# Gate tiles 2 to 7 of the linear-attention branch in three pairs of seven products

## The chip, the cores and the metric

The kernel runs on one core of a Trainium2 chip. The metric is the device time of one execution in microseconds (us); the figure given for a kernel is the median of several executions. Besides, one execution is recorded by the hardware profiler: its span runs from the first to the last instruction, and the trace lists every instruction of the five engines with start and duration: TensorE (PE, its weight loads apart as PEld), VectorE (DVE), ScalarE (ACT), GpSimd (POOL) and SyncE (SP, which issues the DMAs).

## The reference, cut to what matters

One layer of a hybrid decoder in fp32, between two half-step SwiGLU networks. The middle part, the mixer, has two branches, linear attention (a) and stick-breaking attention (b):

```
proj = u @ w_in                       # u: 560 tokens x 1024
q_a, k_a, v_a, gk_low, r_a, q_b, k_b, v_b, gate_a, gate_b = jnp.split(proj, offs, axis=-1)
...
o_a = rms_norm(o_a, gla_norm_g).reshape(B, L, V_GLA).astype(x.dtype) * jax.nn.silu(r_a)
...
o_b = sb_attend(q_b, keys, vals, sb_bias, q_off).reshape(B, L, SB_W)
m = jax.nn.sigmoid(gate_a) * (o_a @ w_o_gla) + jax.nn.sigmoid(gate_b) * (o_b @ w_o_sb)
h = h + rms_norm(m @ w_out, mix_post_g)
```

The change concerns `r_a`, 1024 columns of `u @ w_in`: the gate of the linear branch. They are computed in eight tiles of 128 columns, r0 to r7, each for all tokens (512 prompt tokens, 32 sample tokens and 16 meta tokens, 560 in all).

## The kernel before

**Products.** Activations lie transposed, 128 features on the partitions and the tokens in two halves, columns of 280 and 264. Every fp32 factor is split into a high part (hi) and the rest (lo), and a product is the sum of hi·hi, hi·lo and lo·hi. A **plain** tile (`tile_steps`, L718) takes 8 steps, one for each 128 rows of the weight, of 6 matmuls (three products, two token halves; lines 728, 729 and 731). A **pair** (`seven_steps`, L1043) computes two neighbouring tiles at once in the manner of Strassen: seven products of half depth and half width in place of eight, each with 4 x 3 matmuls, so 84 matmuls in 14 steps where two plain tiles take 96 in 16 (lines 1079, 1080 and 1081). Its four accumulators a, d, b and c are all the PSUM banks for such products. In between, intermediate sums are carried over: ACT copies a to b (L1069) before the third product, which is the first to use b, later b to c (L1069 again), and to SBUF (L1059).

**Weights.** A weight arrives by DMA as `raw`, ACT casts it to `hi` (L1006 or L706), DVE subtracts to get `lo` (L172 with `lo<-raw,hi`). A pair needs sums of weight quarters besides: `weights_at` (L1036) sets four DVE additions of 128x512 (`weight_sums`) 10, 10, 9 and 8 steps before the pair, and the parts b1, t, b2 and t4, each a cast and a subtraction, from 6 steps before to 6 steps after its beginning (b1 4 and 3 steps before when a pair stands ahead of it).

**What follows a gate tile.** `gate_r` (L2358), after a plain tile: the attention output `o` comes back from DRAM, ACT takes the sigmoid of both accumulators (L2371), DVE multiplies (`by`, three L172), then `o` is split: a cast on ACT (L2345) and a subtraction on DVE. `r_pair` (L2384) does the same for a pair at steps 13 to 16 after its beginning (`by_t`, `by_sg`; ACT lines 2399, 2414, 2403 and 2345). All split `o` are the input of the tiles o0 to o7 (`out_a`).

**Order.** Each engine executes its instructions in the order in which the program emits them. The list `MIXER` (L44) gives the order of the mixer's tiles, "R" for a plain tile, "S" for a pair. A counter of steps runs along, and other work hangs on fixed steps: `later(n, f)` emits f n steps further on, `when(n, f)` at an absolute step. The first 24 steps run inside `attention`, among the pieces for the last pair of heads: scores (L2010), scans (L2027), weighing (128x1343, L172), copies of the turned weights (L2089 on PE, L2092 on ACT) and sums (L2105). Steps after those are laced with the sample tokens' attention: keys turned (L2192 on PE, L2194 on ACT), products (L2206, L2239, L2293, L2308), and softmax pieces on DVE (L2252, L2253, L2277, L2278). All those are at fixed step numbers, whichever tile runs there. SBUF is an arena of rooms whose places are read from the table `PLACES`, one byte for each taking; an instruction that writes a room taken over waits for those that used it last.

Of the kernel before, what the change touches and what calls it, by code (L numbers as in the profile page):

```python
# [18 lines left out]
KD = D // P  # L19
# [31 lines left out]


PLACES = bytes.fromhex("""
1e1218555a06420c505e52908e8070488a7a7e667668946a3264868c4c7c6038842a883462283c742672240a544e6e000292042c4a6c78823e2c
103c383a363047412d54565a0a5808443e424660067c8c0c34882c4c26247262842a742e1e0200146e824a786c123016921a36226a664890947a
32683c8e1e1880408a5a701003254e64277e86360e1a050428761b3e8a1f3a2318535c1c64360265700019260c0d4e1b017176283b5a64180038
3924231e0270190c1a36770d4e1876535b04013822715a5d641f1e0c1a707718100219384e712176645c1e0c5a702353100077183971763b6421
1e0c4e705323105a380c1a717776183a64651e23703818534e100e0c7684946c90788e6458468274167c7a4c500a88183c123008684a8c442c48
2e9270747a242a361e2c004c5a5d4823502e2036424b222a1e214b4d222a4c202d50511e4b5150224d1f201e212400301e50181c224b38373b36
393a19181b82667468603c5c14123e160690625a42501c442e4618887a84802d1b7e76947857153f6961673d928c0a72221e08200d4a13758317  # L60
49704c484b4d5d548e865c8a6e566a0e2d6c0c2c7c401910645570801a2a18847a54585c57562d888978795494725856768c0a2c187e9220221e
0428887824269046003234304e743a6862186053146612023b364a4c3f3e0848162c8209395c1e9238787e2a5a3626765618424c3c245d685428
4a60538c48666394881a14623f3e3a72501c22291e045d926078384a30342a2c7e58680a234e905c486654823a8c08282409636294885b551674
4604480032222047535a3e601e7802382e4a50665d429236194e3a5c764c9063088c82091c625e5672943c745b182e3846025406287e78926636
262458304c4a6888901676631214343a5b4e2b193802302a4e460a08573644555854423a3430061902265b2b425534522438503b262a060a5430
1b364e3a02192450570844425b2b19364e3402525618080a4630242e26292a2c4250380654025b1942242e34572938521a1c2c36024e30502a06
0a2d5b5d083418582c2a42245b072e38245256291c1806342a503a02542608240a4e3028504345341a3628065b2b4e420a303a0656072c2a3738
241c1934265402283a0845365c305e432e1a24454e37075b30585642062a2c1843191b4536383a5434025e5c1d4f565158282e0a0618424e5b08
0230024345560642262434580a36545c5e3a381c34360a1a58062e2c3a184f515e06323058011a54004a4c5c185e5a76622a28604a44423a3856
3e4e460234081c62560a60763663064a4c32625c525036185a5e320002463a441d08364a38421c4c345c0604621c080676604c56440a185c3a5a  # L70
1c0832065e424438585c08301a360a3a4c1c4656544b1a3208344a5d5c3022061e5848204a4442385c3a340b1a460a44080642304c1c32480a1e
203a54585632481a4a2c34634476602a246150280a26020462060801004460522200762e30634c1c02184e3e5a604246621a4a4c635e004d0405
18026260364b44764a4d395a18006e64108a1612687c787e6a740c7a408e8c88707284576726941e926d3406083266800a2c4a37829150140e4c
668648206c54828356242a28903a36573c8c60623e3d662d82804a37670822762c6e8e64661e339226670635949532080b8872706655847a0774
54610c0d41403f7e68426f0a778d658f46588a0706080b16124f747c3830548a104c3a780e423648866c267a142a9084822e5a1a24804a7e7288
683462662c2001187092527658604e5450563e466e0c7a5b8e1d65641a1e1c8c320822245a4243065f7a943d0402203c46181c26648f451e0008
225c1a03441f4006233c0a8f478e2028642400422202441c433c40235a03041a64245d0b5c0a461e5f42008f8e653e5a3d20040b64400226245c
4625416544428f3c0a8e40210222645c0425652400448f3c208e47400a0241465c5d5e24648e668874606c386834842e7e8a042c901800200e76
3c827c5430620a48725c0846108636784e5e06042818261e015c245a064600035c25282700245a05290403260424030025292826274206544e04
40033e241d28041a3c002c52137a8c18261c  # L80
""")


class Arena:
# [52 lines left out]
def hybrid_step(  # L137
# [15 lines left out]
    V, S, G, T = nc.vector, nc.scalar, nc.gpsimd, nc.tensor  # L153
# [64 lines left out]
    r = 0  # L218
# [47 lines left out]
    W1 = NP + NS - HW  # L266
# [452 lines left out]
    def tile_steps(act, w1, order=range(KD)):  # L719

        wid = (HW, w1)
        hi, lo = st.parts.pop(0)
        acc = {h: ps("acc") for h in range(2)}
        for k in order:
            a = {h: act.get(k, h, wid[h]) for h in range(2)}
            for h in range(2):
                w = HW if k == order[0] else wid[h]
                T.matmul(acc[h][:, :w], hi[k], act.get(k, h, w)[0], start=(k == order[0]), stop=False, skip_group_check=True)  # L728
# [36 lines left out]
    def later(n, f):  # L765
        todo.append([n, f])
# [748 lines left out]
    with tc.manual_schedule(engines={E.PE, E.DVE, E.Activation, E.Pool}):  # L1515
# [262 lines left out]
        for e in range(2):  # L1778
            acc = {h: ps("acc") for h in range(2)}
# [14 lines left out]
        for j in range(5):  # L1794
            n = P if j < 4 else NTL
# [31 lines left out]
        for hd, head in enumerate(HEADS):  # L1827
# [10 lines left out]
            for c in range(2):  # L1838
# [495 lines left out]
    oas, oap = Parts(), []  # L2334
# [163 lines left out]
    with tc.manual_schedule(engines={E.PE, E.DVE, E.Activation, E.Pool}):  # L2498
        kps, mixer_at, at = {}, {}, {}

        def when(n, f, *args):
            mixer_at.setdefault(n, []).append((f, args))
# [54 lines left out]
        for pr in range(8):  # L2557
            now, n, after = Pair(pr), BEGIN[pr + 1], BEGIN[pr + 2] if pr < 7 else BEGIN[8] + 18
# [25 lines left out]
        n, w0 = BEGIN[8], Weights(0)  # L2584
# [16 lines left out]
        n = 0  # L2601
# [29 lines left out]
        n = 8 * len(PAGES)  # L2631
# [43 lines left out]
        n = 0  # L2675
# [18 lines left out]
        for i, (n, h) in enumerate([(n, 0) for n in range(8)] + [(n, 1) for n in range(7, -1, -1)]):  # L2694
# [12 lines left out]
            acc = product(ms, (h,), held[n])  # L2707
# [94 lines left out]
```

## Time and profile before

| | |
|---|---|
| median of 3 executions | 1482.21 us (1482.03 to 1482.53) |
| the profiled execution's own time | 1483.2 us |
| its span | 1481.5 us |
| mean granted TensorE clock | 0.999 |
| ACT busy | 818.8 us (55%) |
| POOL busy | 86.6 us (6%) |
| r0, r1, r2 and r7 begin | 777.7, 789.1, 800.6 and 811.9 us |
| pairs r3 and r5, tile o0 begin | 820.4, 835.4 and 850.3 us |

The profiled execution took 1.0 us more than the median, and its span leaves out 1.7 us of it. The gate tiles occupy 778 to 850 us; the last pieces of attention run among them up to about 812 us. In the listings a time is the start in us from the span's beginning; then follow the length, engine, line, operation, output and inputs, the tile's shape, and in brackets how long the engine had stood idle and for what. Rows of matmuls overlap each other: their pitch, not their length, is what one costs.

### The profile page before, as it was taken

How to read it: one execution, taken by the hardware profiler on the slowest of the kernel's cores; microseconds unless marked ns; L12 is line 12 of the kernel's file. 1: busy time of each engine (PE TensorE's matmuls, PEld its weight loads, DVE VectorE, ACT ScalarE, POOL GpSimd, SP SyncE). 2: the span in 40 equal slices, each digit the busy share in tenths (PEclk: the TensorE clock that was granted, in tenths of full speed). 3: DMA queues.
4: the chain of work that ended last, by engine and by line, in shares of the span. 5: the costliest groups of instructions: out<-in, count | busy, mean ns of one | idle time of the engine just before them, and what ended most of it. 6: DMA issues, size and time to landing. Idle time of an engine off the chain costs nothing.

```text
span 1481.5 us, 29805 instructions
## 1 busy us (share of the span) xinstructions
PE 1472.6 (99%) x11825; PEld 1426.8 (96%) x11825; DVE 1097.5 (74%) x1844; ACT 818.8 (55%) x1537; POOL 86.6 (6%) x175
## 2 busy tenths in 40 slices
PE   9999999999999999999999999999999999999998
PEld 8999999999999889999998999999999999999998
DVE  5888888855677866988887754776577888889544
ACT  7455545533565557777776544644564554545334
POOL 2000000000000111412211000000000000000000
PEclk9999999999999999999999999999999999999999
DMA  8133333324665787568687757335531333333243
GB/s 254 44 100 92 100 94 100 90 79 128 179 133 130 180 164 162 115 116 154 148 141 168 238 130 212 100 93 156 164 104 51 104 95 110 96 104 88 85 141 123
DMA packets 288541, 187.61 MB, mean 127 GB/s; under 512 B 10988, under 2 KB 266674, under 8 KB 288402
## 3 DMA queue, kind: packets, MB, share of 16 engines
q1 hardware_dynamic: 280706, 181.97, 46.5%
q0 software_dynamic: 7680, 3.74, 2.3%
q8 instruction: 93, 1.52, 0.4%
q14 instruction: 46, 0.38, 0.1%
q10 hardware_dynamic: 16, 0.00, 0.0%
HBM read 160.63 MB, written 25.03 MB: 125 GB/s over the span
## 4 chain that ended last, share of the span: by engine, by line
PE 95%; DVE 2%; ACT 1%; DMA 1%; issue 0%; DVEq 0%; SPq 0%; ACTq 0%
PE acc L1302 8%; PE acc L1301 8%; PE acc L1300 8%; PE acc L741 7%; PE acc L744 6%; PE acc L742 6%; PE acc L728 5%; PE acc L729 5%; PE acc L731 5%; PE acc L1079 4%; PE acc L1081 4%; PE acc L1080 4%; PE acc L1242 2%; PE acc L1239 2%; PE acc L1240 2%; PE ps L2105 1%
## 5 line engine op out<-in xcount | busy, mean ns | idle before, releaser
L172 DVE TENSOR_TENSOR room<-room,room 128x560 fp32r<-128x560 f32 (+14 forms) x464 | 300.9, 667 | 85.2 <-ACT room L1059 17.7
L172 DVE TENSOR_TENSOR lo<-raw,hi 128x1024 fp32r<-128x1024 f32 (+1 forms) x207 | 248.6, 1202 | 76.6 <-ACT hi L1006 39.3
L1302 PE MATMUL acc<-room,lo 128*128 128x280 f32 (+1 forms) x896 | 259.6, 290 | 0.0
L1300 PE MATMUL acc<-room,hi 128*128 128x280 f32 (+1 forms) x896 | 259.1, 289 | 0.0
L1301 PE MATMUL acc<-room,hi 128*128 128x280 f32 (+1 forms) x896 | 259.1, 289 | 0.0
L1006 ACT CAST hi<-raw 128x1024 fp32r<-128x1024 f32 x114 | 119.5, 1052 | 143.5 <-PE acc L1301 49.0
L728 PE MATMUL acc<-room,hi 128*128 128x280 f32 x608 | 173.1, 301 | 0.3 <-DVE room L175 0.3
L1300 PEld LDWEIGHTS acc<-room,hi 128*128 128x128 f32 x896 | 168.8, 188 | 0.0
L1302 PEld LDWEIGHTS acc<-room,lo 128*128 128x128 f32 x896 | 168.7, 188 | 0.0
L1301 PEld LDWEIGHTS acc<-room,hi 128*128 128x128 f32 x896 | 168.5, 188 | 0.0
L729 PE MATMUL acc<-room,hi 128*128 128x280 f32 x608 | 163.5, 288 | 0.0
L1079 PE MATMUL acc<-room,hi 128*128 128x280 f32 x476 | 141.7, 298 | 1.1 <-ACT acc L1069 1.0
L172 DVE TENSOR_TENSOR lo<-room,hi 128x1024 fp32r<-128x1024 f32 x106 | 101.2, 955 | 53.0 <-ACT hi L1006 52.8
L1081 PE MATMUL acc<-room,lo 128*128 128x280 f32 (+1 forms) x476 | 138.5, 291 | 0.0
L1080 PE MATMUL acc<-room,hi 128*128 128x280 f32 (+1 forms) x476 | 138.2, 290 | 0.0
L706 ACT CAST hi<-raw 128x1024 fp32r<-128x1024 f32 (+1 forms) x93 | 93.6, 1007 | 77.6 <-issue 20.4
L1006 ACT CAST hi<-room 128x1024 fp32r<-128x1024 f32 x106 | 89.1, 840 | 81.7 <-PE acc L1301 60.6
L731 PE MATMUL acc<-room,lo 128*128 128x280 f32 x608 | 125.7, 288 | 0.0
L728 PEld LDWEIGHTS acc<-room,hi 128*128 128x128 f32 x608 | 114.4, 188 | 5.3 <-issue 3.9
L729 PEld LDWEIGHTS acc<-room,hi 128*128 128x128 f32 x608 | 114.6, 188 | 0.3
L741 PE MATMUL acc<-room,hi 128*128 128x280 f32 (+2 forms) x388 | 110.7, 295 | 0.0
L742 PE MATMUL acc<-room,hi 128*128 128x280 f32 (+2 forms) x388 | 108.8, 290 | 0.0
(412 smaller groups left out, 3588.2 us busy)
## 6 DMA issues: line engine op xcount, KB each, us to landing
raw<-in_w_in_dram SPq DMA_DIRECT2D x68, 256.0 KB, 5.2
raw<-in_ffn_w_gate_dram SPq DMA_DIRECT2D x64, 256.0 KB, 3.1
raw<-in_ffn_w_up_dram SPq DMA_DIRECT2D x64, 256.0 KB, 3.3
raw<-in_ffn_w_down_dram SPq DMA_DIRECT2D x36, 448.0 KB, 3.8
raw<-in_w_in_dram SPq DMA_DIRECT2D x29, 512.0 KB, 6.9
out_dram<-room SPq DMA_DIRECT2D x36, 256.0 KB, 4.0
room<-in_cache_k_dram SPq DMA_DIRECT2D x32, 256.0 KB, 5.1
room<-in_cache_v_dram SPq DMA_DIRECT2D x32, 256.0 KB, 5.9
```

Of the source, the lines that this page charges most:

```text
L172: (eng or V).tensor_tensor(out=out, in0=a, in1=b, op=op)
L728: T.matmul(acc[h][:, :w], hi[k], act.get(k, h, w)[0], start=(k == order[0]), stop=False, skip_group_check=True)
L729: T.matmul(acc[h][:, : wid[h]], hi[k], a[h][1], start=False, stop=False, skip_group_check=True)
L731: T.matmul(acc[h][:, : wid[h]], lo[k], a[h][0], start=False, stop=(k == order[-1]), skip_group_check=True)
L741: T.matmul(acc[h][:nw, : wid[h]], wh, a[h][0], start=(k == 0), stop=False)
L742: T.matmul(acc[h][:nw, : wid[h]], wh, a[h][1], start=False, stop=False)
L1006: S.copy(hi[:, :kt], src)
L1079: T.matmul(x[:, :n], hi, act_[k][0][:, :n], start=(first and k == 0), stop=False, skip_group_check=True)
L1081: T.matmul(x[:, :w], lo, act_[k][0][:, :w], start=False, stop=(k == 3), skip_group_check=True)
L1300: T.matmul(x[:, :QW], hi, act[k][0], start=(first and k == 0), stop=False, skip_group_check=True)
L1301: T.matmul(x[:, :QW], hi, act[k][1], start=False, stop=False, skip_group_check=True)
L1302: T.matmul(x[:, :QW], lo, act[k][0], start=False, stop=(k == 3), skip_group_check=True)
```

## The change

The list `MIXER` now begins with r0 and r1 plain and three pairs, r2 with r3, r4 with r5 and r6 with r7; before it was r0, r1, r2 and r7 plain and two pairs, r3 with r4 and r5 with r6. The gate tiles take 16 + 42 = 58 steps where they took 32 + 28 = 60. Two further lines follow from that: o0 takes its eight inputs in another order, so that those of the last pair come last, and the second halves of the normed input's rooms are given back at the beginning of r2's pair. `PLACES` is replaced as a whole: from the first byte on, tiles lie in other rooms.

```
-MIXER = [("R", "r", 0), ("R", "r", 1), ("R", "r", 2), ("R", "r", 7), ("S", "r", 3), ("S", "r", 5)]
+MIXER = [("R", "r", 0), ("R", "r", 1), ("S", "r", 2), ("S", "r", 4), ("S", "r", 6)]
...
 PLACES = bytes.fromhex("""
-1e1218555a06420c505e52908e8070488a7a7e667668946a3264868c4c7c6038842a883462283c742672240a544e6e000292042c4a6c78823e2c
+2a005a300e38084434161254701a806a72784a487c18267e944c64625666884e8e527a6e608c1f281c8a680c0d3682923c403e4e6c905824204e
...
-        acc = yield from tile_steps(oas, W1, (0, 1, 2, 7, 3, 4, 6, 5) if n == 0 else range(KD))
+        acc = yield from tile_steps(oas, W1, (0, 1, 2, 3, 4, 5, 7, 6) if n == 0 else range(KD))
...
-        when(starts["r", 3], halved)
+        when(starts["r", 2], halved)
```

What moves on the engines is seen at three places. The names in the rows: `raw`, `hi` and `lo` are weights, `acc` the accumulators, `ps` other PSUM tiles, `room` a place of the arena; in brackets stands which engines or DMA queues the instruction waits for.

The first place is DVE while r1 runs, from the `lo` of r1's weight to the weighing of the last but one head. Before:

```order
L172 TENSOR_TENSOR lo_9276<-raw_8897,hi_9275 128x1024 [waits DMAHW2_49,PE_49,Activation_49]
L2027 SCALAR_TENSOR_TENSOR room_81_4592<-room_81_4592,room_103_5552 128x400
L2027 SCALAR_TENSOR_TENSOR room_81_4592<-room_81_4592,room_103_5552 128x528 [waits Activation_49]
L2027 SCALAR_TENSOR_TENSOR room_5_73<-room_5_73,room_103_5552 128x144 [waits Activation_49]
L172 TENSOR_TENSOR room_76_4272<-acc_9223,room_76_4272 128x280 [waits Activation_49]
L172 TENSOR_TENSOR room_76_4272<-acc_9224,room_76_4272 128x264 [waits Activation_49]
L172 TENSOR_TENSOR room_131_7980<-room_131_7980,room_76_4272 128x544 [waits DMAHW5_49,DVE_49]
L172 TENSOR_TENSOR room_139_9071<-room_139_9071,room_81_4592 128x1343 [waits Pool_49]
```

And now:

```order
L172 TENSOR_TENSOR lo_9275<-raw_8894,hi_9274 128x1024 [waits DMAHW2_49,PE_49,Activation_49]
L172 TENSOR_TENSOR room_131_7063<-raw_9201,raw_9040 128x512 [waits DMAHW7_49,DMAHW1_49]
L172 TENSOR_TENSOR raw_9040<-raw_9040 128x512 [waits DMAHW0_49,DVE_49]
L172 TENSOR_TENSOR room_131_7063<-raw_9201,raw_9040 128x512 [waits DMAHW3_49,DVE_49,PE_49]
L2027 SCALAR_TENSOR_TENSOR room_84_4595<-room_84_4595,room_92_5119 128x400
L2027 SCALAR_TENSOR_TENSOR room_84_4595<-room_84_4595,room_92_5119 128x528 [waits Activation_49]
L172 TENSOR_TENSOR room_9_112<-raw_9201,room_131_7063 128x512 [waits DMAHW4_49,DMAHW0_49,DMAHW6_49,DVE_49,PE_49]
L2027 SCALAR_TENSOR_TENSOR room_74_4270<-room_74_4270,room_92_5119 128x144 [waits Activation_49]
L172 TENSOR_TENSOR room_85_4596<-acc_9222,room_85_4596 128x280 [waits DMAHW6_49,DMAHW5_49,Activation_49]
L172 TENSOR_TENSOR room_85_4596<-acc_9223,room_85_4596 128x264 [waits Activation_49]
L172 TENSOR_TENSOR room_108_5557<-room_108_5557,room_85_4596 128x544 [waits DMAHW6_49,DVE_49]
L172 TENSOR_TENSOR room_105_5535<-room_105_5535,room_84_4595 128x1343 [waits Pool_49]
```

The four sums for the pair at r2 now stand between the scans and ahead of r0's three multiplications and the weighing, in a queue that held none of them there.

The second place is ACT a few steps into r2, around the copies of the last head's turned weights (L2092). Before:

```order
L2092 COPY room_133_8271<-ps_9476 128x512 [waits DMAHW4_49,PE_49]
L2092 COPY room_5_73<-ps_9482 128x384 [waits DVE_49,PE_49]
L2092 COPY room_5_73<-ps_9487 128x384 [waits PE_49]
L2371 ACTIVATE room_135_8642<-acc_9342 128x280 [waits DMAHW7_49]
L2371 ACTIVATE room_135_8642<-acc_9343 128x264
L2092 COPY room_139_9071<-ps_9532 128x512 [waits PE_49,Pool_49]
```

And now:

```order
L1006 CAST hi_9465<-room_131_7063 128x1024
L2092 COPY room_131_7063<-ps_9484 128x512 [waits DVE_49,PE_49]
L2092 COPY room_65_3345<-ps_9490 128x384 [waits DMAHW4_49,PE_49]
L2092 COPY room_99_5423<-ps_9495 128x384 [waits DMAHW3_49,PE_49]
L1006 CAST hi_9510<-raw_9201 128x1024 [waits DMAHW7_49,DMAHW0_49]
L2371 ACTIVATE room_9_112<-acc_9345 128x280 [waits DMAHW5_49]
L2371 ACTIVATE room_9_112<-acc_9346 128x264
L1069 COPY acc_9515<-acc_9513 128x280 [waits DVE_49,PE_49]
L2092 COPY room_131_7063<-ps_9549 128x512 [waits PE_49]
```

The first copy now writes the room of the pair's weight sum t, so it comes after the `lo` of t on DVE (which reads that room, and follows the last head's weighing there). A cast of 128x1024 and the pair's copy of a to b have come in ahead of the copy from ps_9549, and the copy of a to b waits for DVE, which still reads that bank for r1's gate.

The third place is ACT where one pair follows on another. Before (r3 to r5), from r3's last copy to the copy of a to b for r5:

```order
L2414 COPY room_103_5552<-acc_9809 128x264 [waits PE_49]
L1006 CAST hi_10003<-raw_9720 128x1024 [waits DMAHW5_49,DMAHW4_49]
L2403 ACTIVATE room_135_8642<-room_103_5552 128x544 [waits Activation_49]
L2345 CAST room_145_10033<-room_131_7980 128x544 [waits DVE_49,Pool_49]
L1069 COPY acc_10008<-acc_10006 128x280 [waits PE_49]
```

And now (r4 to r6; the like stands between r2 and r4):

```order
L2414 COPY room_141_9719<-acc_9802 128x264 [waits PE_49]
L1006 CAST hi_9998<-raw_9735 128x1024 [waits DMAHW7_49,DMAHW0_49]
L2403 ACTIVATE room_84_4595<-room_141_9719 128x544 [waits Activation_49]
L2194 COPY room_75_4271<-ps_10017 128x512 [waits PE_49]
L2194 COPY room_75_4271<-ps_10023 128x512 [waits PE_49]
L2345 CAST room_145_10036<-room_85_4596 128x544 [waits DVE_49]
L1069 COPY acc_10003<-acc_10001 128x280 [waits PE_49]
```

The chain ahead of the copy is the same, with two key copies more in it; it stands at two places now in place of one.

More of the change, by code (lines that the diff above doesn't have):

```diff
@@ L58 @@
[L58 to L77, printed above, removed]
@@ L78 @@
-4625416544428f3c0a8e40210222645c0425652400448f3c208e47400a0241465c5d5e24648e668874606c386834842e7e8a042c901800200e76
-3c827c5430620a48725c0846108636784e5e06042818261e015c245a064600035c25282700245a05290403260424030025292826274206544e04
-40033e241d28041a3c002c52137a8c18261c
+2a005a300e38084434161254701a806a72784a487c18267e944c64625666884e8e527a6e608c1f281c8a680c0d3682923c403e4e6c905824204e
+4213748476860c154f220a38061e100e4e0c6266208856446e8c607a30528e081c28688a2a3e3c908292246c58000204862b5c3684761a542674
@@ new lines @@
+4c187c6438427e4a794e528071785a13953c402c447215316a3a37483e5c3879734f80327850422b2a702d30154494716b145e4e3b365a795c2f
+80525d2a42787071145094364413796a3a465e5a728095782e2a14367094436a3a2c815a5e15446b782e45361372736a9442715a806b15793a5e
+783644726a73705c9536136b943a785a8180157270447305006a9436383a78688860746e4c647a80627c6c03139286548c1e0c728a2670062428
+1a3432306c4e18461c022a44278013812546425a19042444244326454702424624424444424547464244434447545a0c2c2a4353181b44464345
+4247194f51703a882282742a36343094386a24407e483c280626805262667c18924f6c8a8c0851354e202123788464861e322d2b4a713b758937
@@ new lines @@
+9513312f832a1503608e026e720b68904d7a764c801a041892131c7c3e4a1566621402080a0b4d4c8d04130a8a84146c640286784c8c5400585a
+5c5e10824e262c0c56042e240e6a2a5288347013209422322b7446423a363b7830444c371f1e545a5134404a7e88704e0882525e64268c740a50
+78028d948a203a10424684366d6c5848142a1e13343c5144023e5a2e4024545c4a8674781f7e2c8c940a8a100e203b4c26373a360c428d13566a
+8b883c0a14523e1e5a590434506c2806947e440e582010705b265e8a648c4e8233020032488316842a6a2e2c4d4c56281f12063a30867e946c08
+38364a42408c70748a786482100c4e165425485b44468413244d320e1f06222042125e4e08288430165b54371f48445d46424e08244d300e3612
@@ new lines @@
+385e5b092846061684323a4e54481f5b36424409260684324d244a3848470712164e0e305c4c1f423654485e163b26060e325b4e42460744124c
+4a092457551684305b5e361f48541228225d24060e3209161f845e07424e465b4457554d36383a1630845e281f48543712442409480630325d84
+4c5b260728164e3a423846364c202224840e26365b541f4212384a06090e304757484c84424e28163a542436565e265c44328446081f485b5424
+361206264c484a088407300e46443a4238284e1656461f4236544484325b5c21163a28380a584414122423064e27822654583a4064365a8c1614
+04345c284a084c8c8249445e0a884838162656221f6436145a4644485c5a88423a405854200a6421381f145a5e5c28084a48203638644c280838
@@ new lines @@
+0a1622565840543a082636065a1f145e4e5c58163a24120a2809264021083a223812161736243e501e5e1416525a583c08225c5d1e3a12385e20
+363e5052140a2826405c245e5a521e2208323a4a48094c82640e8c88841404653012164244083836320a843a6431654234228850081e203e5446
+64653032443f4254640a064e3e08425035512a3054101a6446704492687a9476781c6e620c006690607e248a747c72806c8648186a8b4a82164c
+4f2853403c3e048b140e8e6c8c4e53525a025e5c282724061e363884084e82168a124b534f88221a3a0a104e187c6a724a4887860c004f53908c
+80744e7e666160486362781d791c6e7a426811013b0b0d4664701b898569284e42202460924a7094265250043e6c140e662c3c025a5c5e8e1632
@@ new lines @@
+562a6a18828a7a6e727e7c12423054806474228c903886361e0646103a58484c350a633c8869001c302b6884852d44781a0c564607634a3e3469
+084b497962883c064254784a33844058082a636968562c89444c78793e420684302e3f8859620a2b544a0878896848474332422a79304c63542e
+6284853e58694488424a68782a633008624b85545643446842843e782e883062893f85544a08433e424446687884889062705c387a6c7c7e3654
+24660872428c8e300e5012046074945e86441e8a82926e3c2220542c06584872562a7442862f2e5654201e21222a1f2375745458201f75231e21
+74224254121e3c74413022873d343f063c26640832868e8c6c
```

3 lines of the change are left out of this document (removed).

## The prediction

> **What bounds the kernel now.** I read the page's list of engines first, then the waits of PE over the whole run, then stretches of 10 us around the gate tiles, and last the rows of PE, DVE and ACT there. The page:
>
> ```profile
> PE 1472.6 (99%) x11825; PEld 1426.8 (96%) x11825; DVE 1097.5 (74%) x1844; ACT 818.8 (55%) x1537; POOL 86.6 (6%) x175
> ```
>
> And the first two groups of PE's waits (in all, times, longest):
>
> ```profile
> PE acc L1533 <- DVE own L276: 1.1, 1, 1.1
> PE acc L1079 <- ACT acc L1069: 1.0, 1, 1.0
> ```
>
> PE sets the time, and in the mixer it waits only once, 1.0 us where pair r5 follows pair r3. So a matmul less is gained in full, and any new wait is paid in full. Whether new waits come depends on the engines beside PE, in the stretches where the change puts work (start:end, then the length, and busy time of PE, PEld, DVE, ACT and POOL; at the end clock, DMA share and GB/s):
>
> ```profile
> 780.00:790.00 10.00, 10.00 (x75) 8.59 (x75) 4.51 (x7) 6.95 (x13) 2.97 (x6) 1.00 0.38 84
> 790.00:800.00 10.00, 10.00 (x88) 9.60 (x90) 8.43 (x16) 6.77 (x12) 1.30 (x6) 1.00 0.83 237
> 800.00:810.00 10.00, 10.00 (x144) 7.88 (x134) 7.79 (x12) 5.89 (x15) 1.62 (x4) 1.00 0.75 184
> 810.00:820.00 10.00, 10.00 (x85) 9.97 (x84) 9.66 (x30) 6.92 (x14) 1.24 (x6) 1.00 0.79 194
> 820.00:830.00 10.00, 10.00 (x124) 9.11 (x123) 9.35 (x21) 4.26 (x9) 0.00 (x0) 1.00 0.95 261
> ```
>
> DVE has some 4 us free between 790 and 810 (20 - 8.43 - 7.79 = 3.8) and almost nothing from 810 to 830. That is where the first of the three pairs now runs, and this is the point on which the forecast turns.
>
> **What PE saves.** Starts of equal steps give the pitch:
>
> ```profile
> 810.40 0.29 PE L728 MATMUL acc<-room,hi 128*128 128x280 f32 x1
> 811.15 0.29 PE L728 MATMUL acc<-room,hi 128*128 128x280 f32 x1
> ...
> 825.35 0.29 PE L1079 MATMUL acc<-room,hi 128*128 128x280 f32 x1
> 826.12 0.29 PE L1079 MATMUL acc<-room,hi 128*128 128x280 f32 x1
> ...
> 829.58 0.28 PE L1079 MATMUL acc<-room,hi 128*128 128x264 f32 x1
> 830.29 0.28 PE L1079 MATMUL acc<-room,hi 128*128 128x264 f32 x1
> ```
>
> A plain step is 811.15 - 810.40 = 0.75, a pair's step 0.77 with 280 columns and 0.71 with 264. A pair has ten of the first and four of the second: 10 x 0.77 + 4 x 0.71 = 10.5; the two plain tiles that it replaces take 16 x 0.75 = 12.0. With the longer first matmul after each interleave I take **-1.3**, between -1.2 (all at 0.77) and -1.5.
>
> **What DVE gets.** One pair more brings four sums (128x512) and the subtractions of t and t4; b1 and b2 stand for the two plain weights' own. The rows of DVE before, around r1 and r2:
>
> ```profile
> 786.61 1.23 DVE L172 TENSOR_TENSOR lo<-raw,hi 128x1024 fp32r<-128x1024 f32 x1 [1.36 <-ACT hi L706]
> 787.76 2.58 DVE L2027 TENSOR_TENSOR_SCAN room<-room,room 128x400 f32<-128x400 f32 x3
> 790.36 0.79 DVE L172 TENSOR_TENSOR room<-acc,room 128x280 f32<-128x280 f32 x2
> 791.19 2.19 DVE L172 TENSOR_TENSOR room<-room,room 128x544 f32<-128x544 f32 x2
> 793.41 0.33 DVE L2038 COPY room<-room 128x96 f32<-128x96 f32 x2
> ...
> 794.37 0.29 DVE L172 TENSOR_TENSOR room<-ps,room 32x128 fp32r<-32x128 f32 x1
> 796.09 0.73 DVE L172 TENSOR_TENSOR room<-room,room 128x544 fp32r<-128x544 f32 x1 [1.43 <-ACT room L2345]
> 796.73 1.60 DVE L2027 TENSOR_TENSOR_SCAN room<-room,room 128x272 f32<-128x272 f32 x2
> ...
> 800.72 1.56 DVE L172 TENSOR_TENSOR room<-room,room 128x1343 f32<-128x1343 f32 x1
> ...
> 809.46 0.69 DVE L172 TENSOR_TENSOR room<-raw,raw 128x512 f32<-128x512 f32 x1 [0.56 <-PE ps L2105]
> ```
>
> A 128x1024 `lo` costs 787.76 - 786.61 = 1.15, a sum about 0.7, so the extra work is 4 x 0.7 + 1.15 + 0.6 = 4.5 us, the last term being t4 with half the columns. It must fit between 787 and 812, where the free time is a handful of short waits for ACT. I follow the queue as it stands now, from the `lo` of r1, which should begin at 786.61 as before: `lo` to 787.8, three sums and the fourth among the scans (2.6 + 2.8) to 793.2, r0's three products and the weighing (0.8 + 2.2) to 796.2, six small copies 1.2 (793.41 to 794.66) to 797.4, `lo` of b1 to 798.5, the split of r0 (0.7) to 799.2 against 796.8 before. Three scans (2.8, which is 796.73 to 800.72 less a `lo` between) to 802.0, the last weighing 1.6 and its copies 0.4 to 804.0, the `lo` of t to **805.1**.
>
> **What waits behind it.** ACT and PE rows of the same place:
>
> ```profile
> 795.92 2.08 ACT L2194 COPY room<-ps 128x512 f32<-128x512 f32 x4
> ...
> 802.37 0.86 ACT L2092 COPY room<-ps 128x384 f32<-128x384 f32 x2 [2.70 <-DVE room L172]
> 803.11 0.70 ACT L2371 ACTIVATE room<-acc 128x280 f32<-128x280 f32 x2
> ...
> 805.40 1.06 ACT L706 CAST hi<-raw 128x1024 fp32r<-128x1024 f32 x1
> ...
> 805.38 0.76 PE L2239 MATMUL ps<-room,room 128*32 128x32 f32 x64
> ```
>
> Two waits are added here. The L2194 copies now write a room that r0's split reads, so they start at 799.2 in place of 795.92, and PE's products with the sample tokens come late by about 2. Then L2092 writes the room of t and waits for its `lo`: 805.1 in place of 802.37. Behind it in ACT's queue: three L2092 (0.52 as each of the four L2194 above, and 0.75 for the two of 384) to 806.4, the cast of b2 (0.95) to 807.3, two sigmoids (0.6) to 807.9, the copy of a to b (0.4), which waits besides for DVE's product on r1's bank (after the `lo` of b2, 807.3 + 1.15 + 0.4 = 808.9) to 809.3, and the next L2092 (0.5) to 809.8. PE's L2239, which the copied weights feed a little further on in PE's queue, cannot pass its own wait for that copy: 809.8 against 805.38, **+4.4**. The bounds: 0, if DVE's short waits take up the 4.5 us, and 5.5, if every one of those hops costs 0.1 more.
>
> **Where pair follows on pair.** Before, that is r3 to r5:
>
> ```profile
> 835.41 0.29 PE L1079 MATMUL acc<-room,hi 128*128 128x280 f32 x1
> ...
> 837.13 0.38 ACT L2414 COPY room<-acc 128x264 f32<-128x264 f32 x1
> ...
> 840.76 0.64 ACT L2345 CAST room<-room 128x544 fp32r<-128x544 f32 x1 [1.75 <-DVE room L172]
> 841.31 0.39 ACT L1069 COPY acc<-acc 128x280 f32<-128x280 f32 x1
> ...
> 841.75 0.40 PE L1079 MATMUL acc<-room,hi 128*128 128x280 f32 x1 [1.00 <-ACT acc L1069]
> ```
>
> The old pair's last gate, sigmoid, product and cast, all stand in ACT's queue ahead of the copy of a to b; that chain takes 841.75 - 835.41 = 6.34 from the new pair's beginning. PE was late by only 1.0 because L2206 and L2293 (1.9 us together) ran among its first four steps. At r4 to r6 those are not there, only one L2192 (0.8): 4 x 0.77 + 0.8 = 3.9 of cover, so PE waits 6.34 - 3.9 = **+2.4**, and the old 1.0 is gone, **-1.0**. At r2 to r4 another wait comes first:
>
> ```profile
> 811.52 0.18 DVE L175 SCALAR_TENSOR_TENSOR room<-room,newm 128x32 f32<-128x32 f32 x1
> 813.21 0.68 DVE L172 TENSOR_TENSOR room<-raw,room 128x512 f32<-128x512 f32 x1
> ...
> 819.82 0.86 DVE L2277 COPY room<-ps 128x32 f32<-128x32 f32 x8
> 820.61 0.27 DVE L2278 COPY room<-ps 32x128 f32<-32x128 f32 x1
> ...
> 821.22 0.64 PE L2308 MATMUL ps<-room 64*32 64x128 f32 x16
> ...
> 823.67 0.40 PE L1079 MATMUL acc<-room,hi 128*128 128x280 f32 x1
> ```
>
> L2308 needs the copy L2278, which before was done 0.34 ahead of it. Now L2278 stands behind r3's first gate product, and that behind the cast of r2's: r2's fifth product ends six steps and some keys (6.5) before r4 begins, and from there stand in a row a copy on ACT (0.4), two subtractions on banks (0.8), two softmax groups (813.21 - 811.52 = 1.7 each), `lo` of b1 and t (2 x 1.15), three products (3 x 0.65), two sets of L2277 and L2278 (819.82 to 820.88, 1.05 each), and two instructions of ACT between (0.9): 11.8. By that count L2278 ends 5 after r4's beginning, and three steps (2.3) are all that PE has before it: **+2.6**; then the copy of a to b for r4 another **+0.4**. The nearest row gives the lower bound: a chain of 6.34 against a cover of four steps and L2308, L2206 and L2293 (2.45, 821.22 to 823.67) gives 0.8 for both.
>
> **The sum**: -1.3 + 4.4 + 2.6 + 0.4 + 2.4 - 1.0 = +7.5 on 1483.2 for the profiled execution, 1490.7; less the 1.0 by which that stood over the median, 1489.7. The hops were all taken as coming one behind the other; where one is off, it will rather be that two waits cover each other, as L2308 does with r4's copy. I forecast **1489**. After o0 nothing gives time back, since PE has no waits there to lose. The new order of o0's inputs costs nothing as long as r6's two splits come within o0's last two steps, six steps (4.5) after its beginning; else the difference. The halved rooms cost nothing, they add no instruction. The new places of the arena add waits anywhere; outside the gate tiles I cost them at nothing, bounded by -0.5 (a wait such as L744's or L872's goes) and +2 (two waits such as r5's come).
>
> **Rivals.**
>
> 1. *DVE takes the sums in its short waits* (the other side: not slower). The place is the `lo` of t; if it ends by 802.4, where L2092 went before, ACT's queue is as early as it was, r4's chain is shorter by as much, and what remains is -1.3 with the wait between pairs twice at 1.0 in place of once: 1483.2 - 1.3 + 1.0 - 1.0 = 1481.9 on the median's scale, down to 1480.9 with both covered. For it: 3.8 us free from 790 to 810, and 5.5 from 780 to 790 if the sums could go there. Against it: they stand behind r1's `lo` at 786.61, which waits for its cast.
> 2. *Only the waits of the pairs come.* The backlog at r2 is eaten by the waits of DVE, but pair on pair is as counted: -1.3 + 0.8 to 3.0 + 2.4 - 1.0 gives +0.9 to +3.1 on the median, 1483.1 to 1485.3.
> 3. *Worse than counted.* From 820 to 830 the DMA queues are at 0.95; the first raw quarters are now fetched earlier and r2's outputs come back in that stretch. A load that lands 2 us late behind r4 gives about 1491.5.
> 4. *The clock.* In every stretch above PE's granted clock is 1.00, and no wait was over 1.1 us. If a wait of 2.6 halved it for as long again, four steps would take 0.77 more each: +2.6, so 1491.6. The Trainium skill (TensorE: Matmul & The Clock Gate, "Why this matters for your kernels") warns of PE idle for more than about 3 us, after which the clock is halved; no run here shows so long a pause yet, and by that rule the waits counted above stay just short of it.
> 5. *The change does not save what it says*: were a pair's steps slower beside the attention pieces (0.80 in place of 0.77), -1.3 would be -0.9; this moves the sum by 0.4.
>
> **Chances.** The forecast (waits of both kinds, 1486 to 1491) 0.53; rival 2 0.2; rival 1 0.13; rivals 3 and 4 together 0.14; rival 5 lies in the range of each. The range must reach into rival 1 and a little beyond the forecast: 1481.3 to 1491.7. About 0.2%, or 3 us, is what a measurement of this kernel can tell from no change: faster is below 1479.2, slower above 1485.2. Faster has 0.03, from rival 1 with a wait lost elsewhere; the rest of rival 1 and most of rival 2 are the same, 0.27; slower 0.7.
>
> **What would show it.** In the trace after: PE's waits should list L2239 or its neighbours behind ACT L2092 at about 806 to 810, L2308 behind DVE L2278, and L1079 behind ACT L1069 two times rather than once; DVE between 790 and 810 near 9.5 of 10; o0 beginning near 857 in place of 850.34. If PE shows no wait between 795 and 810, rival 1 or 2 holds, and my count of DVE's queue is wrong. If waits stand there but the total is 1482, something later gave time back. A granted clock under 1.00 after a wait speaks for rival 4.

## The result, and the profile after

The changed kernel takes 1493.54 us (median of 6 executions, 1491.82 to 1494.75) where the kernel before took 1482.12 beside it: the ratio is 1.0076, with a 95% interval of 1.0063 to 1.0089. It is slower by 11.4 us; the forecast was 1489, and the range ended at 1491.7. The profiled execution took 1491.82, with a span of 1490.1 and a mean granted clock of 0.998. The page's list of engines:

```profile
PE 1474.0 (99%) x11813; PEld 1426.2 (96%) x11813; DVE 1102.1 (74%) x1850; ACT 821.7 (55%) x1544; POOL 87.7 (6%) x175
```

PE has 12 matmuls less and yet is busy for 1.4 us longer than before (1472.6). The span grew by 8.6, so that the other 7.2 are new idle time. The waits of PE say where (in all, times, longest):

```profile
PE acc L1079 <- ACT acc L1069: 2.5, 1, 2.5
PE ps L2308 <- DVE room L2278: 2.1, 1, 2.1
PE ps L2239 <- ACT room L2092: 1.8, 1, 1.8
...
PE ps L2192 <- DVE room L172: 0.8, 1, 0.8
...
PE ps L2089 <- ACT room L2092: 0.7, 1, 0.7
PE ps L2089 <- ACT room L2194: 0.5, 1, 0.5
```

These six are 8.4 us, all in the gate tiles, where there was one of 1.0. The stretches of 10 us (PE, PEld, DVE, ACT and POOL; at the end clock, DMA share and GB/s) show the rest:

```profile
790.00:800.00 10.00, 8.73 (x70) 8.17 (x68) 9.83 (x18) 4.94 (x9) 0.91 (x3) 1.00 0.52 137
800.00:810.00 10.00, 7.49 (x64) 6.04 (x64) 8.10 (x11) 6.05 (x13) 0.11 (x1) 1.00 0.80 228
...
820.00:830.00 10.00, 7.90 (x94) 6.94 (x96) 8.97 (x29) 5.90 (x11) 0.11 (x1) 1.00 0.72 210
830.00:840.00 10.00, 9.98 (x103) 9.56 (x93) 8.06 (x14) 5.69 (x12) 0.00 (x0) 1.00 0.67 215
840.00:850.00 10.00, 7.50 (x59) 6.21 (x61) 5.57 (x7) 6.22 (x13) 0.22 (x2) 0.86 0.82 257
```

DVE is full from 790 to 800 (9.83, 8.43 before) and PE loses 1.3 there and 2.5 in the next stretch. From 840 to 850 PE loses 2.5 by waiting, and besides its granted clock falls to 0.86. The rows of the engines around the waits, in order of time:

```profile
799.25 2.05 ACT L2194 COPY room<-ps 128x512 f32<-128x512 f32 x4 [4.13 <-DVE room L172]
...
803.76 1.22 DVE L172 TENSOR_TENSOR lo<-room,hi 128x1024 fp32r<-128x1024 f32 x1
805.07 1.35 ACT L2092 COPY room<-ps 128x512 f32<-128x512 f32 x3 [2.83 <-DVE lo L172]
...
809.07 0.38 ACT L1069 COPY acc<-acc 128x280 f32<-128x280 f32 x1 [1.12 <-DVE room L172]
810.00 0.76 PE L2239 MATMUL ps<-room,room 128*32 128x32 f32 x64 [1.77 <-ACT room L2092]
...
828.07 0.27 DVE L2278 COPY room<-ps 32x128 f32<-32x128 f32 x1
828.49 0.42 PE L2308 MATMUL ps<-room,room 64*32 64x128 f32 x8 [2.10 <-DVE room L2278]
...
846.52 0.39 ACT L1069 COPY acc<-acc 128x280 f32<-128x280 f32 x1
846.96 0.40 PE L1079 MATMUL acc<-room,hi 128*128 128x280 f32 x1 [2.50 <-ACT acc L1069]
847.19 0.35 PE L1080 MATMUL acc<-room,hi 128*128 128x280 f32 x1
847.35 0.43 PE L1081 MATMUL acc<-room,lo 128*128 128x280 f32 x1
847.58 0.43 PE L1079 MATMUL acc<-room,hi 128*128 128x280 f32 x1
847.81 0.43 PE L1080 MATMUL acc<-room,hi 128*128 128x280 f32 x1
```

The chain at r2 is the one that the prediction followed, hop for hop: the L2194 copies start at 799.25 (799.2 was counted), the `lo` of t ends at 803.76 + 1.22 = 804.98 (805.1), L2092 starts at 805.07, and PE's L2239 at 810.00 (809.8). L2308 waits behind L2278, and r6's product behind the copy of a to b. The last rows show what the sum did not have: from 847.35 on a matmul takes 0.43 in place of 0.29, and the next starts 0.23 later in place of 0.13. In pieces of 1 us the granted clock is:

```profile
847.00:848.00 1.00, 1.00 (x5) 1.00 (x6) 0.37 (x1) 0.74 (x2) 0.00 (x0) 0.63 0.88 252
848.00:849.00 1.00, 1.00 (x11) 0.51 (x13) 0.00 (x0) 0.00 (x0) 0.00 (x0) 0.50 1.08 338
849.00:850.00 1.00, 1.00 (x16) 0.43 (x12) 0.00 (x0) 0.00 (x0) 0.00 (x0) 0.50 0.96 347
850.00:851.00 1.00, 1.00 (x28) 0.85 (x24) 0.59 (x1) 0.00 (x0) 0.00 (x0) 0.66 0.58 162
```

The clock is halved for (0.37 + 0.50 + 0.50 + 0.34) x 2 = 3.4 us, a stretch of half clock from here on. PE does half as much in them, so they cost 1.7 us. They follow PE's longest wait, 2.5 us.

### The profile page after: what moved, and what is told of

Read it like the earlier page. It is cut to its first block, busy times and chain, and to the rows that moved or that the text cites. A ratio compares the mean times of both kernels' runs of the same rounds, so it can differ in the third digit from the quotient of the medians.

```text
span 1490.1 us, 29766 instructions
## 1 busy us (share of the span) xinstructions
PE 1474.0 (99%) x11813; PEld 1426.2 (96%) x11813; DVE 1102.1 (74%) x1850; ACT 821.7 (55%) x1544; POOL 87.7 (6%) x175
## 4 chain that ended last, share of the span: by engine, by line
PE 94%; DVE 3%; ACT 2%; issue 1%; DMA 1%; DVEq 0%; SPq 0%; ACTq 0%
PE acc L1302 8%; PE acc L1300 8%; PE acc L1301 8%; PE acc L741 6%; PE acc L742 6%; PE acc L744 6%; PE acc L728 5%; PE acc L729 4%; PE acc L731 4%; PE acc L1079 4%; PE acc L1081 4%; PE acc L1080 4%; PE acc L1239 2%; PE acc L1242 2%; PE acc L1240 2%; DVE room L172 1%
## 5 line engine op out<-in xcount | busy, mean ns | idle before, releaser
L172 DVE TENSOR_TENSOR room<-room,room 128x560 fp32r<-128x560 f32 (+13 forms) x471 | 304.8, 665 | 75.3 <-ACT room L808 17.0
L1302 PE MATMUL acc<-room,lo 128*128 128x280 f32 (+1 forms) x896 | 259.8, 290 | 0.0
L1301 PE MATMUL acc<-room,hi 128*128 128x280 f32 (+1 forms) x896 | 259.5, 290 | 0.0
L1300 PE MATMUL acc<-room,hi 128*128 128x280 f32 (+1 forms) x896 | 259.5, 290 | 0.0
L1300 PEld LDWEIGHTS acc<-room,hi 128*128 128x128 f32 x896 | 168.7, 188 | 0.0
L1301 PEld LDWEIGHTS acc<-room,hi 128*128 128x128 f32 x896 | 168.5, 188 | 0.0
L728 PE MATMUL acc<-room,hi 128*128 128x280 f32 x576 | 164.0, 301 | 0.2 <-DVE room L175 0.2
L729 PE MATMUL acc<-room,hi 128*128 128x280 f32 x576 | 155.1, 289 | 0.0
L1079 PE MATMUL acc<-room,hi 128*128 128x280 f32 x504 | 150.8, 299 | 2.5 <-ACT acc L1069 2.5
L1081 PE MATMUL acc<-room,lo 128*128 128x280 f32 (+1 forms) x504 | 146.7, 291 | 0.0
L1080 PE MATMUL acc<-room,hi 128*128 128x280 f32 (+1 forms) x504 | 146.3, 290 | 0.0
L731 PE MATMUL acc<-room,lo 128*128 128x280 f32 x576 | 119.1, 288 | 0.0
L728 PEld LDWEIGHTS acc<-room,hi 128*128 128x128 f32 x576 | 108.4, 188 | 4.7 <-issue 3.4
L729 PEld LDWEIGHTS acc<-room,hi 128*128 128x128 f32 x576 | 108.5, 188 | 0.2
```

Of the source, the lines that this page charges most:

```text
L172: (eng or V).tensor_tensor(out=out, in0=a, in1=b, op=op)
L1079: T.matmul(x[:, :n], hi, act_[k][0][:, :n], start=(first and k == 0), stop=False, skip_group_check=True)
L1080: T.matmul(x[:, :w], hi, act_[k][1][:, :w], start=False, stop=False, skip_group_check=True)
L1081: T.matmul(x[:, :w], lo, act_[k][0][:, :w], start=False, stop=(k == 3), skip_group_check=True)
L1300: T.matmul(x[:, :QW], hi, act[k][0], start=(first and k == 0), stop=False, skip_group_check=True)
L1301: T.matmul(x[:, :QW], hi, act[k][1], start=False, stop=False, skip_group_check=True)
```

## The experiments

Theory at this point: each of PE's waits is paid in full, every one has the cause that the prediction gave it, and a wait that is long enough halves the clock for 3.4 us on top. Rivals: the waits are symptoms of one backlog on DVE and go or stay together; or the clock's fall has nothing to do with them. The runs undo one cause each, then all; two add a pause to the kernel before, and the last two go on from the run that undoes all. Where an edit moves the taking of rooms, `PLACES` is adapted in the few bytes that it needs (5 to 35 of 1533).

**The changed kernel again**, unedited, for the spread and for a second profile.

> The changed kernel once more, unaltered, for a second profile. In the first profile TensorE waited 7.4 us in six places between 797 and 847 us and its clock was at half from 847.3 to 850.7 us; that execution took 1491.8, the median of six 1493.5. Theory A, the clock falls to half for stretches of 3.4 us that cost 1.7 each, and how many there are differs from execution to execution: the same waits within 0.3 each, a whole number of half-clock stretches after waits, and a span that is longer by 1.7 for each stretch more. Theory B, the waits themselves differ: the same one stretch, and one of the waits longer by what the span is longer.

1492.74 (1492.27 to 1493.82; ratio 1.0072, 1.0059 to 1.0086). Its profile has the same six waits (0.8, 0.5, 0.7, 1.8, 2.1, 2.5) and one stretch of half clock, again 3.41 us long and again behind the wait of 2.5. It stands 0.9 above the profile shown, and 0.7 of that arises in the first 40 us of the run, where L1614 waits 1.3 in all in place of 0.8. So these two executions differ by waits, as the second of the two theories had it, and not by one more stretch.

**The weight sums of r2's pair three steps earlier**, ahead of r1's `lo`, where DVE has time (4.51 busy of 10 from 780 to 790).

```
-weights_at(when, n, (what, t), b1=...)
+weights_at(when, n, (what, t), (-13, -13, -12, -11) if i == 2 else (-10, -10, -9, -8), b1=...)
```

> The four weight sums for the pair at r2 three steps earlier, into the time in which VectorE stood idle from 780 to 786 us. Theory A, the four waits around r2 (0.8 + 0.5 + 0.7 + 1.8 = 3.8) come from VectorE being late by those sums: they shrink to under 1.5 in all, the lo of t ends near 802.5 in place of 805.0, the time falls by about 3, and the waits of L2308 and L1069 stay at 2.1 and 2.5. Theory B, the waits come from the rooms that the copies reuse, whatever VectorE's load: 3 or more of the 3.8 stay. Theory C, the raw quarters land too late: VectorE waits for a DMA at the sums and r1's lo comes later than 786.4.

1489.81 (1488.41 to 1491.28; 1.0049, 1.0036 to 1.0063). The waits of 0.8, 0.5 and 0.7 are gone; L2239's 1.8, L2308's 2.0 and L1069's 2.5 stay. The four waits at r2 come to 1.8, a little over the 1.5 expected. So the waits don't go together: three hang on the sums, the others have causes of their own. The clock behaves in a way that neither theory had. PE's rows in this run:

```profile
807.52 0.76 PE L2239 MATMUL ps<-room,room 128*32 128x32 f32 x64 [1.77 <-ACT room L2092]
...
809.09 0.43 PE L1080 MATMUL acc<-room,hi 128*128 128x280 f32 x1
...
847.27 0.40 PE L1079 MATMUL acc<-room,hi 128*128 128x280 f32 x1 [2.51 <-ACT acc L1069]
847.50 0.29 PE L1080 MATMUL acc<-room,hi 128*128 128x280 f32 x1
847.63 0.29 PE L1081 MATMUL acc<-room,lo 128*128 128x280 f32 x1
```

And its clock in pieces of 1 us:

```profile
808.00:809.00 1.00, 1.00 (x35) 0.96 (x25) 0.26 (x1) 1.00 (x3) 0.00 (x0) 0.75 0.86 210
...
829.00:830.00 1.00, 1.00 (x28) 1.00 (x20) 0.77 (x2) 0.20 (x1) 0.00 (x0) 0.50 0.85 204
```

After the wait of 1.77 matmuls take 0.43, at half clock; after the longer wait of 2.51 they take 0.29. A rule by the length of the pause alone can't give that. But the clock falls at 808.50 and, after L2308's wait, at 828.98, which is 20.48 later, six times 3.413. Counted on in steps of 3.413, a stretch begins at 846.05 and cuts the pause of 2.51 (844.76 to 847.27) into 1.29 and 1.22. The wait of 1.77 lay whole in one stretch.

**The last gate part of r2 and r4 one step later** (`by_sg(0)` at 17), so that the copy of a to b does not stand behind it.

```
-..., (15, lambda: by_t(0)), (16, lambda: by_sg(0))):
+..., (15, lambda: by_t(0)), (17 if n < 6 else 16, lambda: by_sg(0))):
```

> In pairs r2 and r4 the last gate product, cast and split one step later, so that the next pair's copy of a to b stands ahead of that cast on ScalarE. Theory A: the wait of 2.5 at r6's third product goes (under 0.3), with it the half clock behind it (1.7): about 4.2 less than the changed kernel; L2308 still waits about 2.1. Theory B, the clock falls for the sum of waits within a stretch and not for this one: 2.5 less, and a half-clock stretch elsewhere.

1490.60 (1488.50 to 1491.82; 1.0053, 1.0039 to 1.0067).

```profile
PE acc L1079 <- ACT acc L1069: 1.1, 1, 1.1
```

The wait behind L1069 falls from 2.5 to 1.1 and not under 0.3, since the parts of r4 before it (a cast, a sigmoid and two key copies) still stand ahead of the copy on ACT. The profile has no half clock behind any wait, though L2239's 1.8 and L2308's 2.1 are still there. The cause is right, the size of what it frees was set too high.

**Both last gate parts later** (16 and 18).

```
-..., (15, lambda: by_t(0)), (16, lambda: by_sg(0))):
+..., (16 if n < 6 else 15, lambda: by_t(0)), (18 if n < 6 else 16, lambda: by_sg(0))):
```

> In pairs r2 and r4 the last tile's first gate product one step later and its second two steps later, so that the copies for L2308 stand ahead of the one and the next pair's copy of a to b ahead of the other. Theory A: both waits go, L2308 to under 0.6 and L1069 to under 0.3, and the half clock with them: 2.1 + 2.5 + 1.7 = about 6 less than the changed kernel, 1487 to 1488; the waits around r2 stay at 3.8. Theory B, something else is late right behind (o0's input, or L2293's pages): less than 4 is gained.

1488.04 (1487.33 to 1488.65; 1.0039, 1.0025 to 1.0053).

```profile
PE acc L1079 <- ACT acc L1069: 1.1, 1, 1.1
...
PE ps L2308 <- DVE room L2278: 0.4, 1, 0.4
```

L2308's wait falls from 2.1 to 0.4, L1069's is 1.1 (under 0.3 was expected), those of r2 stay at 3.8, and there is no half clock. Both handovers from pair to pair were late because of the gate parts queued ahead of them.

**The sums earlier, and other rooms** for two tiles (the sample keys, and the turned weights that lay in the room of t). Only bytes of `PLACES` differ from the second run, 12 of them: these two, and ten by which other tiles make way:

```
room of the turned weights: 56 -> 78
room of the sample keys:    70 -> 58
```

> As e2 (sums for r2 three steps earlier), and the first of the last head's turned weights and the sample keys ahead of it lie in other rooms of the arena, so that L2092 no longer writes the room of the pair's sum t. In e2 L2239 still waited 1.8, and L2092 still stood 2.8 for the lo of t. Theory A, that room is the cause: the 2.8 on ScalarE goes, the wait of L2239 falls under 0.8, the time falls by 1.0 to 1.8 against e2, by more where the clock fell for that wait. Theory B, r1's gate product (behind the lo of b2 on VectorE, ahead of the copy of a to b on ScalarE) keeps it: L2239 waits 1.5 or more as before.

1488.59 (1487.39 to 1489.32; 1.0043, 1.0029 to 1.0057). No wait is left at r2: L2239 too needed the room, besides the sums. L2308's 2.1 and L1069's 2.5 remain, and one half-clock stretch follows the 2.5. That is the prediction's own separation: the waits at r2 come from the sums and the arena, those between pairs from the gate parts.

**All of it**: the sums earlier, the rooms, the part b2 of r2 a step later, and gate parts at (12, 13, 16, 18) for r2 and (13, 14, 17, 18) for r4.

```
+for d, f in zip((6,) + {2: (12, 13, 16, 18), 4: (13, 14, 17, 18), 6: (13, 14, 15, 16)}[n], (load, ...)):
+weights_at(..., (-13, -13, -12, -11) if i == 2 else (-10, -10, -9, -8), b1=..., b2=(0, 2 if i == 2 else 1))
```

> All of it together: sums for r2 earlier, other rooms for the turned weights and keys, the lo of b2 for r2 behind r1's gate product, r2's gates at steps 12, 13, 16 and 18 and r4's at 13, 14, 17 and 18 in place of 13 to 16. If the waits that were counted are the whole of the loss, no wait over 0.8 is left from 790 to 850, the clock stays whole, and the plain gain of the third pair shows: 1.3 to 1.5 under the kernel before, near 1481. Rival: other waits come up behind those that are taken away, and it stays 2 or more over the kernel before.

1482.71 (1482.32 to 1483.09, 11 executions; 1.0004, 0.9995 to 1.0013), no different from before. Of the 11.4 us nothing is left. The 1481 that was expected is not reached, for PE's rows still have two waits in the gate tiles, this one and L1079's of 0.6:

```profile
821.39 0.42 PE L2308 MATMUL ps<-room,room 64*32 64x128 f32 x8
823.00 0.42 PE L2308 MATMUL ps<-room,room 64*32 64x128 f32 x8 [1.19 <-DVE room L2278]
```

**A pause put into the kernel before**: for the copy of a to b at r5, ACT makes the same copy 3 times, or 6 times. Everything else is as it was, so this tests the clock by itself.

```
-(2, lambda: S.copy(b[:, :HW], a[:, :HW])),
+(2, lambda: [S.copy(b[:, :HW], a[:, :HW]) for _ in range(3 if f == ("r", 5) else 1)]),
```

> The kernel before, with the copy of a to b for r5 done three times in place of once, so that its wait of 1.0 grows to about 1.6. In the traces so far the clock went to half for 3.4 us behind each stretch of 3.413 us on a fixed grid in which TensorE stood idle for 1.95 us or more, never for 1.70 or less, and for 1.77 in one of three. Theory A, the idle share of such a stretch decides: no half clock, 0.6 more than the kernel before in every execution. Theory B, a pause as such drops the clock: some executions 2.3 more.

> The kernel before, with that copy done six times, so that the wait grows to about 2.5. Theory A: where the grid leaves 1.8 or more of the pause in one stretch (about 7 of 10 executions) the clock is at half for 3.4 us and the time is 1.5 + 1.7 = 3.2 more than before; where it cuts the pause in the middle, 1.5 more. Theory B, the half clock of the changed kernel came from something else (its load): 1.5 more always.

PE's rows with the shorter pause, and then with the longer:

```profile
842.57 0.40 PE L1079 MATMUL acc<-room,hi 128*128 128x280 f32 x1 [1.82 <-ACT acc L1069]
842.80 0.29 PE L1080 MATMUL acc<-room,hi 128*128 128x280 f32 x1
```

```profile
843.00 0.40 PE L1079 MATMUL acc<-room,hi 128*128 128x280 f32 x1 [3.05 <-ACT acc L1069]
843.24 0.29 PE L1080 MATMUL acc<-room,hi 128*128 128x280 f32 x1
...
844.04 0.44 PE L1080 MATMUL acc<-room,hi 128*128 128x280 f32 x1
...
847.48 0.29 PE L1080 MATMUL acc<-room,hi 128*128 128x280 f32 x1
```

The long pause, 3.05 in place of the 2.5 expected, halves the clock from 843.98 to 847.39, 3.41 us again, and not from the end of the pause: behind the first matmul, of 0.40, five more run at 0.29. The kernel takes 1485.84 (1484.30 to 1486.92; 1.0024, 1.0014 to 1.0033), 3.5 above before: 2.0 of longer wait (3.05 against 1.0) and some 1.5 of clock. The short pause shows no half clock in its profile and takes 1483.54 (1482.49 to 1485.49; 1.0011, 1.0002 to 1.0020). Its 11 executions fall into two groups, six from 1482.49 to 1483.54 and five from 1484.38 to 1485.49, with 0.84 us of nothing between. A wait longer by 0.8 explains the first group (1482.3 + 0.8 = 1483.1); the second stands some 1.7 higher, the price of one stretch. The mean granted clock of each execution bears this out: 0.998 in all five of the second group, 0.999 or 1.000 in the six of the first and in all 26 of the kernel before beside them. With the long pause it is 0.997 or 0.998 in nine executions of ten, and 0.999 in the fastest, which at 1484.30 has the longer wait alone (1482.3 + 2.0). That the pause fell otherwise on the grid in these executions fits, but only one execution of each kernel has a profile.

**Two attempts to get below the kernel before.** In the run with everything, two of DVE's instructions for r2's gate, a product and the subtraction of the split, stand ahead of the second L2278. Here they go behind it, first for r2 alone, then for r4 too:

```
-{2: (12, 13, 16, 18), 4: (13, 14, 17, 18), ...
+{2: (13, 17, 16, 18), 4: (13, 14, 17, 18), ...
...
+{2: (13, 17, 16, 18), 4: (13, 17, 16, 18), ...
```

> As e6_all, and r2's gate parts stand at (13, 17, 16, 18) in place of (12, 13, 16, 18), so that DVE has its two sums on sg's half a behind both L2278 copies of L2278's second half and not ahead of them. Theory (each wait of PE is paid in full, and no others are there): the wait of the second half of L2308, 1.2 in e6_all, falls under 0.4, L1069's stays under 1.2, no half clock, and the time falls by 0.8 to 1.2 from e6_all's 1482.7, to 1481.5 to 1481.9, that is 0.4 to 0.8 below before, which is what the seven products save less what is left of the waits. Rival (DVE has no more room around the pair and something else comes late): another wait of 1 or more comes up between 825 and 850 and the time is 1482.3 or more.

> As e9_sums_behind_copies, and r4's gate parts stand at (13, 17, 16, 18) too in place of (13, 14, 17, 18): L1069's copies of r4 then come behind fewer gate casts on ACT. Theory: L1069's wait, 0.6 in e6_all, falls under 0.3 and the time by another 0.3 to 0.6 below e9_sums_behind_copies. Rival: r4's sums now stand closer to r6's use of its rooms, the wait moves to r6 (behind 850) and the time is within 0.3 of e9_sums_behind_copies or above it.

The first takes 1481.91 (1480.93 to 1482.45; 0.9995, 0.9986 to 1.0004) and the second 1480.98 (1479.94 to 1481.69; 0.9991, 0.9982 to 1.0000), beside 1482.41. The second gains 0.9 on the first, more than the 0.3 to 0.6 expected. In the first L2308's wait is gone and L1069's is still 0.6; in the second both are. The page of the second, and its stretches of 10 us:

```profile
PE 1471.5 (99%) x11813; PEld 1426.1 (96%) x11813; DVE 1101.9 (74%) x1850; ACT 822.0 (56%) x1544; POOL 89.8 (6%) x175
```

```profile
800.00:810.00 10.00, 9.87 (x141) 7.62 (x134) 8.67 (x14) 6.88 (x17) 0.11 (x1) 1.00 0.69 185
...
820.00:830.00 10.00, 10.00 (x124) 9.05 (x123) 9.96 (x23) 4.42 (x10) 0.11 (x1) 1.00 0.98 288
...
840.00:850.00 10.00, 10.00 (x93) 9.80 (x83) 5.06 (x9) 4.46 (x11) 0.11 (x1) 1.00 0.67 216
```

PE is busy throughout but for 0.13 in the first of these, with DVE at 9.96 of 10 from 820 to 830. That is the change without its waits. PE's busy time is 1.1 below before (1471.5 against 1472.6), which is what the third pair saves. By the medians it is 0.1% faster, at the edge of what can be told from no change.

## Why the prediction was wrong

The direction, the places and nearly all sizes of the waits were right. What failed is a term that stood among the rivals and was put at nothing in the sum: the clock after a wait, 1.7 us in the profile. It is not the whole of the distance, since with 1.7 more the forecast would have been 1490.7; what is left of it stays open (below).

- **PE's saving, -1.3**: 1.1, by PE's busy time in the last run.
- **r2, +4.4**: L2239 runs 4.6 later than before (810.00 against 805.38), for the reasons that the prediction gave: three of its waits went with the sums (second run), the last with the rooms (fifth). The idle time listed is only 3.8. The other 0.8 is in PE's restarts: the ten L2089 behind a wait take 1.42 up to the next group (799.98 to 801.40), 0.24 more than before (798.45 to 799.63), and the listed idle time counts from the last matmul's end, 0.29 after its start, while the next would have started after 0.13.
- **r2 to r4, +2.6 and +0.4**: L2308 waits 2.1 (the prediction's own hops, 11.8 - 6.5 - 2.3, come to 3.0 and not 2.6), and the copy of a to b is then hidden, as "it will rather be that two waits cover each other" had it.
- **r4 to r6, +2.4**: 2.5. The old **-1.0** is gone as counted.
- **The sum of these**, +7.5, comes out as 4.6 + 2.1 + 2.5 - 1.0 - 1.1 = +7.1.
- **The clock: the step that failed.** Rival 4 named the mechanism and had its mark (a clock under 1.00 after a wait), but it shared 0.14 with rival 3 and was left out of the sum, though the sum itself contained a wait of 2.4 and one of 2.6. The price was tied to the pause ("as long again"), and its working does not come out: four steps at 0.77 more each are 3.1, not 2.6. The runs show a fixed stretch of 3.41 us, at 1.7 each. And the point from which it decides was set too high: 1.77 us of idle time in one stretch was enough in the second run (L2239). The Trainium skill (TensorE: Matmul & The Clock Gate, "What's actually happening") describes a free-running window of 3413 ns, and the clock's falls in the second run, 20.48 = 6 x 3.413 apart, agree. The same section of the Trainium skill gives one idle window of about 3.4 us as the condition, and there the second run's 1.77 decides against it; the prediction had taken from the Trainium skill's rule of about 3 us that its waits stay "just short of it".
- **The rest of the median.** The profiled execution, with one stretch, took 1491.82; the median is 1.7 above. One more stretch in most executions would give just that, since the changed kernel has three waits of 1.8 to 2.5 and it depends on the grid which of them count. The granted clocks show it for some executions only: of the eleven that the changed kernel has in all, two (1493.31 and 1493.46) have 0.997, as the second run's profile with its two stretches; eight have 0.998, as the changed kernel's two profiles with one stretch each, and one (1492.27) has 0.999. The second of these profiles is the median of its five, 1492.74. Nor is the clock all that varies: in the third run 1488.50 and 1490.60 both have 1.000. L1614, in the first 40 us, waits 0.4 in each of the three profiles of the kernel before (two of them with a pause), and 0.4 to 1.4 in the nine of the changed kernel and its variants, whose arena is new; whether the new places do that or chance does, no run tells. So the rest stays open.
- **Rivals 1 and 2**: DVE's free time from 790 to 800 was indeed used up (9.83 in place of 8.43), and it was not enough; the `lo` of t ended 2.6 behind rival 1's mark of 802.4. **Rival 3**: the trace has no wait of an engine for a load from 812 to 858.
- **The signs**: L2239, L2308 and L1079 wait behind what was named, but L1079 once and not twice, as r4's copy is hidden; and DVE is busy for 17.93 of the 20 us from 790 to 810, 9.0 of 10 in place of the 9.5 expected.

For the profiled execution the terms give 7.1 + 1.7 = 8.8, less the wait of 0.5 at L744 that the profiled execution of before had and the one after has not: 8.3 of the 8.6 us. That 0.5 may be part of the 1.0 that the forecast took off to get from its profiled execution to the median. It took the changed kernel's profiled execution to stand as far above its median; it stood 1.7 below.

## What to carry to other kernels

With PE busy for 99% of the span, following each engine's queue hop by hop, with the rows' own durations, placed each new wait of 1.8 us or more, and gave the delay behind it to within 0.5 us. To the sum of the waits belongs the clock: in this kernel a single wait of PE near 2 us or more is to be priced at its length plus 1.7 us times the chance that it lies mostly in one stretch. And a change that moves work by steps needs the fixed step numbers, the rooms and the gate parts around it set anew: with the same three pairs the time went from 1493.5 to 1481.0, as only the places of other work and of tiles were changed.

## What the hardware showed that was not expected

The clock is granted in stretches of 3.41 us on a grid of its own. In all profiles here, with the grid counted from that run's fall of the clock, a stretch with 1.77, 1.95, 2.44 or 2.50 to 2.51 us of PE idle was followed by one stretch at half clock, and none with up to 1.70 was (1.55 and 1.65 in the changed kernel's second profile, 1.49 and 1.70 in its first, 1.68 with the short pause). In the third and fourth runs, whose grid is counted back from the clock's fall at the end of the run, as it is with the short pause, 1.78 was not. So the point lies near 1.8, a little over half a stretch, and the position of a wait on the grid, which differs between executions, decides as much as its length. With the short pause that made one kernel's times fall into two groups some 1.7 us apart, and the mean granted clocks with them.
